# Stick-breaking attention: the mask's products ahead of the scores', and one product for two sums

## The chip, the cores and the metric

One core of a Trainium2 chip runs the whole program. The metric is device time in microseconds (us) of one execution, the median of several runs; lower is better. TensorE (PE in the profile) does matrix products, VectorE (DVE) and ScalarE (ACT) work on elements, GpSimd (POOL) does some element work and issues some transfers, SyncE (SP) issues the others. PSUM is the memory that TensorE writes its sums to, in banks of 512 fp32 columns.

## The reference

Two layers of a transformer-like trunk over 512 frames and 16 meta tokens of width 1024: half a SwiGLU, then a mixer (stick-breaking attention with 8 heads of 64 beside a convolution branch), then half a SwiGLU. The change touches the attention alone:

```python
def stick_breaking_attention(q, k, v):
    """A[t,s] = sigmoid(z_ts) * prod_{s<j<t} (1 - sigmoid(z_tj)), s < t."""
    ...
    def block(args):
        qb, start = args
        z = jnp.einsum('bhqd,bhkd->bhqk', qb, kh) * scale
        qpos = start + jnp.arange(Q_BLOCK, dtype=jnp.int32)[:, None]
        valid = key_pos < qpos
        log_keep = jnp.where(valid, jax.nn.log_sigmoid(-z), 0.0)
        after = lax.cumsum(log_keep, axis=3, reverse=True) - log_keep
        attn = jnp.where(valid, jnp.exp(jax.nn.log_sigmoid(z) + after), 0.0)
        return jnp.einsum('bhqk,bhkd->bhqd', attn, vh)
```

## The kernel before, in words

Activations lie with channels on the 128 partitions and the 528 tokens along the columns. Large fp32 products are made of three products of parts: a number is split into a rounded part and a rest (`qh`, `ql`), and high by high, high by rest and rest by high are summed in PSUM.

The mixer of a layer takes the heads in four pairs, `attend(i, ...)`. While a pair is worked on, TensorE's gaps are filled with the projections that come next: `attend` is a generator, and at each of its `yield`s the loop around it puts half of a projection (24 products of `by_halves`, line 700) into TensorE's stream. That engine's order is fixed by the order of the calls (`tc.manual_schedule`). The other engines' instructions are ordered by the framework, by priority.

The 528 keys are the 512 of four blocks of 128 (t = 3, 2, 1, 0) and the last 16, which are handled apart, as a corner. For one pair `attend` does, in TensorE's order:

- the corner: scores of the 16 last keys with the 16 last queries (and of the first 16 keys with the first 16 queries, in the layer that keeps the meta tokens) in the tile `zs` of 64 used rows: rows 0 to 15 for the pair's first head, rows 32 to 47 for its second; their softplus is `e4` (64x32);
- at line 895 a product of `e4` with the first 128 columns of the constant `l4` adds the sums over later keys to `zs`, and puts the first head's total over the 16 keys into row 127 (column 127 of `l4` is -1 for that head); at line 896 a second product, with the other 128 columns of `l4`, puts the second head's total into row 127 of columns 32 to 47 and nothing else; a copy on DVE (line 900) takes rows 96 to 127 of both to the tile `corner`;
- `scores(t, ...)` four times, for pieces 3, 2, 1 and 0 of the keys, with 256, 272, 400 and 512 queries: the three products of parts for each of the two heads (line 852), and then for each head the mask's product (line 855), identity by a bf16 mask of 240, 128, 128 and 112 columns. The softplus follows on ACT and DVE, and for t = 3 `corner` is subtracted (line 862). In the text these are the first, second, third and fourth piece;
- between them other products: line 907 (`vb` by `a4`, after the first piece, only where the meta tokens are kept), line 919 (the same two operands' corner values, right ahead of the third piece), the sums over later blocks (lines 874 to 877) and the values (line 892).

A head is 64 channels, so the score products contract over 64 rows: the first head of the pair lies on partitions 0 to 63, the second on 64 to 127. The trace writes such a product as 64*128 (64 rows by 128 columns of the array) and one that uses all rows as 128*128. The products of lines 895, 896, 907 and 919 are plain fp32, contract over partitions 0 to 63, and show as two passes each. The mask's product is 128*128, as are the projections.

All constants come in one tile `cc`; `l4` is a view of it in the kernel before (line 297). `constants()` copies others of them to tiles of their own, at a late priority. A PSUM accumulation starts with the product that has `start=True`; the later ones of the same bank add to what has been written since, and overwrite elsewhere.

Of the kernel before, what the change touches and what calls it, by code (L numbers as in the profile page):

```python
# [7 lines left out]
F32 = mybir.dt.float32  # L8
# [5 lines left out]
P = 128  # L14
# [40 lines left out]
C_L4 = 496  # L55
# [5 lines left out]
def kernel(ctx, tc, hT, par, const, wg1, wu1, wd1, win, wao, wco, wout, wg2, wu2, wd2, out):  # L61
    nc = tc.nc
    act, dve, pool, pe = nc.scalar, nc.vector, nc.gpsimd, nc.tensor

    cst = ctx.enter_context(tc.tile_pool(name="cst", bufs=1))
# [11 lines left out]
    def split(x, hi, lo):  # L77

        act.copy(hi, x)  # L79
        dve.tensor_tensor(out=lo, in0=x, in1=f(hi), op=ALU.subtract)  # L80

    @contextmanager
    def priority(offset):

        old = tc.cur_priority
        tc.cur_priority = max(0, old + offset)
        yield
        tc.cur_priority = old
# [7 lines left out]
    def fn(out, in_, func, **kw):  # L96
        need = SETS[func]
        if table["set"] != need:
            load = act.preload_act_table_set(need)
            for p in table["acts"]:  # L100
                tc.add_manual_dep(load.ins, p.ins.name, NOSYNC, reason="table order")
            table.update(set=need, load=load, acts=[])
        i = act.activation(out, in_, func, **kw)
        tc.add_manual_dep(i.ins, table["load"].ins.name, NOSYNC, reason="table order")
        table["acts"].append(i)
# [137 lines left out]
    def unit(*key):  # L243
        while state["prep"] < min(len(units), state["use"] + 1 + LOOK):
            if units[state["prep"]][2] in QUAD and quads["pool"] is None:
                break
            prep_unit()
        assert units[state["use"]][0] == key, (units[state["use"]][0], key)
        state["use"] += 1
        return ready.pop(key)  # L250
# [25 lines left out]
    cc = cst.tile([P, N_CONST], F32, name="cc")  # L276
# [6 lines left out]
    identb = cst.tile([P, P], BF16, name="identb")  # L283
    maskb = cst.tile([P, 240], BF16, name="maskb")
    masksb = cst.tile([64, 32], BF16, name="masksb")

    def constants():

        nc.sync.dma_start(prm[:, N_NORM:], par[:, N_NORM:])
        nc.sync.dma_start(cc, const)  # L290
        with priority(LATE):
            dve.tensor_copy(trir, cc[:, C_TRI:C_TRI + P])
            dve.tensor_copy(identb, ident)
            dve.tensor_copy(maskb, cc[:, C_MASK:C_MASK + 240])
            dve.tensor_copy(masksb, cc[:64, C_MS:C_MS + 32])

    l4 = cc[:64, C_L4:C_L4 + 2 * P]
    bias = cst.tile([P, 4], F32, name="bias")
    pool.memset(bias[:, 0:1], 1e-6)
    pool.memset(bias[:, 1:2], 1e-5)  # L300
# [153 lines left out]
    def ffn(l, fi, st, mode, after):  # L454
# [3 lines left out]
        with tc.tile_pool(name=f"ffn{l}{fi}", bufs=1, reuse_waits="tile") as fp, \  # L458
# [53 lines left out]
            def first_head():  # L512
# [5 lines left out]
                for a, b in BEGIN:  # L518
                    for k in range(a, b):
                        prepare(fp, k, 0, st, alloc="later")  # L520
                    for raw, (hi, lo) in zip(begin, ws):
                        split(raw[:, a:b], hi[:, a:b], lo[:, a:b])
                    for k in range(a, b):
                        squares(fp, k, st, mode)
                    if b == KD:
                        fetch()
                        fetch_sums()
                        constants()
                        norm["r"] = rms_rstd(fp, st, ptile("pe"), mode)
                    for k in range(a, b):  # L530
                        xh, xl = st["u"][k]
                        for ps, (hi, lo) in zip(pss, ws):
                            for pi, (wt, xt) in enumerate(((hi, xh), (hi, xl), (lo, xh))):
                                for e, s in enumerate(toks):
                                    pe.matmul(ps[:, e, :TH], wt[:, k, :], xt[:, s], start=(k == 0 and pi == 0),
                                              stop=(k == KD - 1 and pi == 2))
# [121 lines left out]
    def mixer(l, st, omode, after):  # L658
        last = omode == XO
        with ExitStack() as es:  # L660
# [8 lines left out]
            def hold(k, width, name):  # L669
                return hpool.tile([P, width], F32R, tag=f"h{k}", bufs=1, name=name)  # L670
# [62 lines left out]
            with tc.tile_pool(name=f"psm{l}", bufs=2, space=bass.MemoryType.PSUM, reuse_waits="tile") as psp, \  # L733
                    tc.tile_pool(name=f"psz{l}", bufs=2, space=bass.MemoryType.PSUM, reuse_waits="tile") as psz:

                def ztile():
                    return psz.tile([P, 2, 512], F32, tag="z", name="z")
# [28 lines left out]
                with tc.tile_pool(name=f"att{l}", bufs=1, reuse_waits="tile") as ap_:  # L766
# [26 lines left out]
                    def softplus(dst, z, np_):  # L793
                        act.activation(dst, z, AF.Abs)
                        fn(dst, dst, AF.Exp, bias=bias[:np_, 3:4], scale=-1.0)
                        fn(dst, dst, AF.Ln, bias=bias[:np_, 2:3], scale=1.0)
                        dve.scalar_tensor_tensor(out=dst, in0=z, scalar=0.0, in1=dst, op0=ALU.max, op1=ALU.add)

                    def attend(i, step, qf, kf, vf):
                        qc = META if last else 0  # L800
                        qh, ql, kh, kl = (hold(n, T, nm) for n, nm in enumerate(("qh", "ql", "kh", "kl")))
# [5 lines left out]
                        w = ncor * 16  # L807
                        zt = ztile()
                        zs, pt = zt[:, 0, :], zt[:, 1, :]
# [7 lines left out]
                        for c, t0 in ((0, SEQ), (1, 0))[:ncor]:  # L817
                            for hh in range(2):
                                r = slice(64 * hh, 64 * hh + 64)
                                pe.matmul(zs[32 * hh:32 * hh + 16, c * 16:c * 16 + 16], kf[r, t0:t0 + 16],  # L820
                                          qf[r, t0:t0 + 16], start=False, stop=False, skip_group_check=True)
                        e4 = ap_.tile([64, 32], F32, tag="e4", bufs=2, name="e4")
# [22 lines left out]
                        def scores(t, q0, n, m0):  # L845
                            z = ztile()
                            ks = slice(t * P, (t + 1) * P)

                            for pi, (kk, qq) in enumerate(((kh, qh), (kh, ql), (kl, qh))):
                                for hh in range(2):  # L850
                                    r = slice(64 * hh, 64 * hh + 64)
                                    pe.matmul(z[:, hh, :n], kk[r, ks], qq[r, q0:q0 + n], start=(pi == 0), stop=False,  # L852
                                              skip_group_check=True)
                            for hh in range(2):
                                pe.matmul(z[:, hh, :240 - m0], identb, maskb[:, m0:], start=False, stop=False,
                                          skip_group_check=True)
                            sp = ap_.tile([P, 2, 512], F32, tag="big", bufs=BIG, name="sp")[:, :, :n]
                            sh, sl = (ap_.tile([P, 2, n], F32R, tag=f"s{x}{t}" if t else "big", bufs=1 if t else BIG,
                                               name=f"s{x}") for x in "hl")
                            softplus(sp, z[:, :, :n], P)  # L860
                            if t == 3:
                                dve.tensor_tensor(out=sp[96:128, :, n - 16:], in0=sp[96:128, :, n - 16:],
                                                  in1=corner[96:128], op=ALU.subtract)
                            split(sp, sh, sl)
                            later[t] = (z, sh, sl, q0, n)
# [26 lines left out]
                                    pe.matmul(po[:, hh, q0 - META:q0 - META + n], v[:, t, hh * P:hh * P + P], p[:, hh, :],  # L892
                                              start=False, stop=(t == 0 and p is al), skip_group_check=True)

                        pe.matmul(zs[:, :w], l4[:, 0:P], e4[:, :w], start=False, stop=True, skip_group_check=True)
                        pe.matmul(zs[:, 32:48], l4[:, P:2 * P], e4[:, :16], start=True, stop=True, skip_group_check=True)
                        fn(a4[:, :w], zs[:64, :w], AF.Exp, bias=bias[:64, 3:4])
                        corner = ap_.tile([P, 2, 16], F32, tag="corner", bufs=2, name="corner")
                        zc = zs[96:128, 0:64].rearrange("p (a b) -> p a b", a=2)[:, :, :16]
                        dve.tensor_copy(corner[96:128], zc)  # L900
                        scores(*PIECES[0])
                        yield
                        step(2)
                        oh = bp.tile([P, T], F32R, tag=f"oh{i}", bufs=1, name="oh")
                        ol = bp.tile([P, T], F32R, tag=f"ol{i}", bufs=1, name="ol")
                        if not last:
                            pe.matmul(zs[:, 64:80], vb[:, 2, :], a4[:, 16:32], start=True, stop=True, skip_group_check=True)
                            with priority(-EARLY):
                                act.copy(oh[:, :META], zs[:, 64:80])
                                dve.tensor_tensor(out=ol[:, :META], in0=zs[:, 64:80], in1=f(oh[:, :META]),  # L910
                                                  op=ALU.subtract)
                        yield
                        scores(*PIECES[1])
                        yield
                        sums_and_weights(3)
                        yield
                        po = psz.tile([P, 2, 512], F32, tag="o", bufs=1, name="po")
                        for hh in range(2):
                            pe.matmul(po[:, hh, 496:512], vb[:, hh, :], a4[:, :16], start=True, stop=False,
                                      skip_group_check=True)  # L920
# [38 lines left out]
                    with tc.manual_schedule(engines={mybir.EngineType.PE}):  # L959
                        for i in range(4):  # L960
                            for _ in attend(i, step, *parts(i)):
                                next(beside, None)
                        for n, fill in enumerate(FILL_END):
                            for _ in range(fill):
                                next(beside, None)
                            step(n)
                        for _ in beside:
                            pass

            with tc.tile_pool(name=f"post{l}", bufs=1, reuse_waits="tile") as pp, \  # L970
# [64 lines left out]
                for jj in range(4):  # L1035
                    w = unit("co", l, jj)
# [85 lines left out]
```

## Time and profile before

| | |
|---|---|
| median of three runs | 2159.0 us (2158.93 to 2159.9) |
| the profiled execution | 2159.58 us |
| its span in the trace | 2157.8 us |
| granted TensorE clock, mean | 0.999 |
| PE busy | 2141.5 us, 99% |
| PEld (weight loads) busy | 2055.4 us, 95% |
| DVE busy | 1521.7 us, 71% |
| ACT busy | 1151.1 us, 53% |
| POOL busy | 485.1 us, 22% |

A record of a product is longer than the distance to the next one, since products overlap in the array; what a product costs in a stream is the distance between starts.

### The profile page before, as it was taken

To read this page: it belongs to the slowest core of one execution; us is meant where nothing else is said; L and a number is where in the kernel's file an instruction comes from. 1 tells how busy PE (TensorE), PEld (TensorE's weight loads), DVE (VectorE), ACT (ScalarE), POOL (GpSimd) and SP (SyncE) were. 2 spreads that over 40 slices of the span, in tenths; PEclk is the share of its full clock that TensorE was granted. 3 is DMA by queue.
4 is the path that set the end of the run, shared out by engine and by line. 5 is a ranking of instruction groups with operands and counts; after the bars stand their busy time and mean duration, and the time that the engine had idled before them with its cause. 6 is when DMAs were issued, how large, how long until landed. Compare 5 with 4: busy or idle time off the path is not lost. (4 is left out here: it accounts for less than half of the span.)

```text
span 2157.8 us, 39881 instructions
## 1 busy us (share of the span) xinstructions
PE 2141.5 (99%) x16242; PEld 2055.4 (95%) x16242; DVE 1521.7 (71%) x2076; ACT 1151.1 (53%) x1590; POOL 485.1 (22%) x429
## 2 busy tenths in 40 slices
PE   9999999999999999999999999999999999999998
PEld 8999999999999999999999999999888879999897
DVE  7867685677766767677877676856677767767685
ACT  6434355477767535343554343554778685444354
POOL 1322321211111131323113223212112111322320
PEclk9999999999999999999999999999999999999999
DMA  8465547865677647464365655368655876665532
GB/s 237 136 166 140 137 107 201 178 133 120 134 171 180 172 129 188 128 164 118 96 171 144 166 143 141 103 197 181 144 123 135 184 184 166 159 177 144 141 111 76
DMA packets 140168, 324.90 MB, mean 151 GB/s; under 512 B 15568, under 2 KB 19664, under 8 KB 139984
## 3 DMA queue, kind: packets, MB, share of 16 engines
q1 hardware_dynamic: 101856, 226.36, 32.9%
q0 software_dynamic: 37440, 95.44, 26.1%
q8 instruction: 127, 2.08, 0.4%
q10 hardware_dynamic: 688, 0.55, 0.1%
q14 instruction: 57, 0.47, 0.1%
HBM read 315.86 MB, written 6.42 MB: 149 GB/s over the span
## 5 line engine op out<-in xcount | busy, mean ns | idle before, releaser
L79 ACT CAST wh<-wr 128x1024 fp32r<-128x1024 f32 (+4 forms) x275 | 243.5, 888 | 377.6 <-PE ps L259 93.5
L80 DVE TENSOR_TENSOR wl<-wr,wh 128x1024 fp32r<-128x1024 f32 (+4 forms) x275 | 300.1, 1094 | 59.0 <-ACT wh L79 55.3
L79 ACT CAST wh<-s 128x1024 fp32r<-128x1024 f32 x158 | 165.8, 1049 | 275.1 <-DVE s L236 91.2
L80 DVE TENSOR_TENSOR wl<-s,wh 128x1024 fp32r<-128x1024 f32 x158 | 214.9, 1360 | 59.5 <-ACT wh L79 58.8
L700 PE MATMUL ps<-uh,wh 128*128 128x264 f32 (+1 forms) x792 | 244.2, 308 | 0.0
L700 PE MATMUL ps<-uh,wl 128*128 128x264 f32 (+1 forms) x792 | 240.0, 303 | 0.0
L700 PE MATMUL ps<-ul,wh 128*128 128x264 f32 (+1 forms) x792 | 239.9, 303 | 0.0
L621 POOL TENSOR_TENSOR h<-h,dt 128x528 f32<-128x528 f32 (+1 forms) x96 | 181.0, 1891 | 256.0 <-DVE dt L619 253.3
L210 POOL DMA_DIRECT2D s<-wg x78 | 74.7, 970 | 592.4 <-DMA s<-wg 202.1
L728 DVE SCALAR_TENSOR_TENSOR y<-uc,prm,y 128x528 f32<-128x528 f32 (+1 forms) x240 | 197.6, 823 | 4.1
L224 ACT CAST wh<-wr 128x1024 fp32r<-128x1024 f32 x104 | 109.1, 1049 | 140.4 <-issue 47.1
L561 PE MATMUL ps<-ul,wh 128*128 128x264 f32 (+1 forms) x624 | 177.4, 284 | 0.0
L561 PE MATMUL pb<-sl,wh 128*128 128x264 f32 (+1 forms) x624 | 176.9, 283 | 0.0
L561 PE MATMUL ps<-uh,wl 128*128 128x264 f32 (+1 forms) x624 | 176.8, 283 | 0.0
L561 PE MATMUL pb<-sh,wl 128*128 128x264 f32 (+1 forms) x624 | 176.8, 283 | 0.0
L561 PE MATMUL pb<-sh,wh 128*128 128x264 f32 (+1 forms) x624 | 176.5, 283 | 0.0
L561 PE MATMUL ps<-uh,wh 128*128 128x264 f32 (+1 forms) x624 | 176.2, 282 | 0.0
L700 PEld LDWEIGHTS ps<-uh,wl 128*128 128x128 f32 x792 | 149.1, 188 | 5.9
L700 PEld LDWEIGHTS ps<-uh,wh 128*128 128x128 f32 x792 | 148.9, 188 | 5.5
L700 PEld LDWEIGHTS ps<-ul,wh 128*128 128x128 f32 x792 | 149.0, 188 | 5.2
L259 PE MATMUL ps<-al,wh 128*128 128x264 f32 (+1 forms) x616 | 142.3, 301 | 0.5 <-DVE al L80 0.2
L259 PE MATMUL ps<-ah,wh 128*128 128x264 f32 (+1 forms) x616 | 141.8, 300 | 0.0
(312 smaller groups left out, 6472.5 us busy)
## 6 DMA issues: line engine op xcount, KB each, us to landing
wr<-wd SPq DMA_DIRECT2D x96, 384.0 KB, 3.4
wr<-win SPq DMA_DIRECT2D x72, 512.0 KB, 4.1
wl<-win POOLq DMA_DIRECT2D x72, 512.0 KB, 7.8
wr<-wg SPq DMA_DIRECT2D x117, 256.0 KB, 3.0
wr<-wu SPq DMA_DIRECT2D x117, 256.0 KB, 3.4
s<-wg SPq DMA_DIRECT2D x78, 256.0 KB, 5.0
s<-wu SPq DMA_DIRECT2D x78, 256.0 KB, 5.6
s<-wg POOLq DMA_DIRECT2D x78, 256.0 KB, 5.4
```

Source lines behind the costliest of these rows:

```text
L79: act.copy(hi, x)
L80: dve.tensor_tensor(out=lo, in0=x, in1=f(hi), op=ALU.subtract)
L210: pool.dma_start(t[:, a:b], src, accum_op=ALU.add)
L224: act.copy(hi[:, :nk], raw[:, :nk])
L259: pe.matmul(ps[:, c, :n], wt[:, k0 + k, :], xt[:, s:s + n], start=(k == 0 and pi == 0), stop=(k == nk - 1 and pi == 2))
L561: pe.matmul(ps[:, e, :TH], wt[:, 4 * e + kk, :], xt, start=start and kk == 0 and pi == 0, stop=kk == 3 and pi == 2, skip_group_check=True)
L621: pool.tensor_tensor(out=tri(h[j], mode), in0=tri(h[j], mode), in1=tri(t, mode), op=ALU.add)
L700: pe.matmul(ps, wt[:, k, :], xt[:, s], start=(n == 0 and pi == 0), stop=(n == KD - 1 and pi == 2))
L728: t = dve.scalar_tensor_tensor(out=y, in0=uc[i][:, c0 + k:k + T], scalar=col(w0 + k), in1=y, op0=ALU.mult, op1=ALU.add)
```

## The change

In `scores` the two mask products now come first and start the accumulation (`start=True`), and the six products of parts add to it. The second product with `l4` is gone: `l4` becomes a tile of 64x128 of its own, a copy of the first 128 columns with column 95 replaced by the second head's column of -1, so that one product leaves the first head's total in row 127 and the second head's in row 95, both in columns 0 to 15. `corner` is then filled by two copies of 32x16, from rows 96 to 127 and from rows 64 to 95. Two copies that build `l4` join `constants()`.

```diff
         with priority(LATE):
             dve.tensor_copy(trir, cc[:, C_TRI:C_TRI + P])
+            dve.tensor_copy(l4, cc[:64, C_L4:C_L4 + P])
+            dve.tensor_copy(l4[:, 95:96], cc[:64, C_L4 + 2 * P - 1:C_L4 + 2 * P])
             dve.tensor_copy(identb, ident)
...
-    l4 = cc[:64, C_L4:C_L4 + 2 * P]
+
+    l4 = cst.tile([64, P], F32, name="l4")
...
-
-                            for pi, (kk, qq) in enumerate(((kh, qh), (kh, ql), (kl, qh))):
+                            for hh in range(2):
+                                pe.matmul(z[:, hh, :240 - m0], identb, maskb[:, m0:], start=True, stop=False,
+                                          skip_group_check=True)
+
+                            for kk, qq in ((kh, qh), (kh, ql), (kl, qh)):
                                 for hh in range(2):
                                     r = slice(64 * hh, 64 * hh + 64)
-                                    pe.matmul(z[:, hh, :n], kk[r, ks], qq[r, q0:q0 + n], start=(pi == 0), stop=False,
+                                    pe.matmul(z[:, hh, :n], kk[r, ks], qq[r, q0:q0 + n], start=False, stop=False,
                                               skip_group_check=True)
-                            for hh in range(2):
-                                pe.matmul(z[:, hh, :240 - m0], identb, maskb[:, m0:], start=False, stop=False,
-                                          skip_group_check=True)
...
-                        pe.matmul(zs[:, :w], l4[:, 0:P], e4[:, :w], start=False, stop=True, skip_group_check=True)
-                        pe.matmul(zs[:, 32:48], l4[:, P:2 * P], e4[:, :16], start=True, stop=True, skip_group_check=True)
+                        pe.matmul(zs[:, :w], l4, e4[:, :w], start=False, stop=True, skip_group_check=True)
                         fn(a4[:, :w], zs[:64, :w], AF.Exp, bias=bias[:64, 3:4])
                         corner = ap_.tile([P, 2, 16], F32, tag="corner", bufs=2, name="corner")
-                        zc = zs[96:128, 0:64].rearrange("p (a b) -> p a b", a=2)[:, :, :16]
-                        dve.tensor_copy(corner[96:128], zc)
+                        for hh in range(2):
+                            dve.tensor_copy(corner[96:128, hh], zs[96 - 32 * hh:128 - 32 * hh, :16])
```

The order on TensorE, in the first layer's second pair. At the first piece, before (`po` is the values' sum of the pair ahead, `z<-e,cc` are the two products with `l4`, x2 is one row for the two heads; the row pair of the mask comes a second time in place of the dots):

```order
L892 MATMUL po<-al,v 128x400
L895 MATMUL z<-e_5746,cc 128x32
L896 MATMUL z<-e_5746,cc 128x16
L852 MATMUL z<-qh,kh 128x256 x2
L852 MATMUL z<-ql,kh 128x256 x2
L852 MATMUL z<-qh,kl 128x256 x2
L855 LDWEIGHTS identb
L855 MATMUL z<-maskb,identb 128x240
...
L700 MATMUL ps<-uh_4162,wh 128x264
```

The same place in the changed kernel (its line 898 is 895 of before, 852 the masks, 858 the products of parts, 895 the values, 703 the projections):

```order
L895 MATMUL po<-al,v 128x400
L898 MATMUL z<-e_5749,l_122 128x32
L852 LDWEIGHTS identb
L852 MATMUL z<-maskb,identb 128x240
...
L858 MATMUL z<-qh,kh 128x256 x2
L858 MATMUL z<-ql,kh 128x256 x2
L858 MATMUL z<-qh,kl 128x256 x2
L703 MATMUL ps<-uh_4165,wh 128x264
```

The second product with `l4` is gone, and the masks stand between the first one and the products of parts.

At the third piece, before, with the corner's values (line 919) ahead of it:

```order
L919 MATMUL po<-a_5747,vb 128x16 x2
L852 MATMUL z<-qh,kh 128x400 x2
L852 MATMUL z<-ql,kh 128x400 x2
L852 MATMUL z<-qh,kl 128x400 x2
L855 LDWEIGHTS identb
L855 MATMUL z<-maskb,identb 128x128
...
L700 MATMUL ps<-uh_4162,wh 128x264
```

The same place now:

```order
L921 MATMUL po<-a_5750,vb 128x16 x2
L852 LDWEIGHTS identb
L852 MATMUL z<-maskb,identb 128x128
...
L858 MATMUL z<-qh,kh 128x400 x2
L858 MATMUL z<-ql,kh 128x400 x2
L858 MATMUL z<-qh,kl 128x400 x2
L703 MATMUL ps<-uh_4165,wh 128x264
```

Here too the masks part two runs of 64*128 products that stood next to each other. At the second and the fourth piece, 128*128 products stand on both sides before and after; there the masks only change sides. The same holds in all four pairs of both layers. On DVE one copy to `corner` has become two in each pair, and two copies join the constants'; the order of ACT, POOL and SP is as before.

## Rows read from the trace of the kernel before

**Rows 1.** The page's part 1: busy time, share of the span, instructions.

```profile
PE 2141.5 (99%) x16242; PEld 2055.4 (95%) x16242; DVE 1521.7 (71%) x2076; ACT 1151.1 (53%) x1590; POOL 485.1 (22%) x429
```

**Rows 2.** Busy us of the engines from 430 to 600 us, and PE's waits there.

```profile
430.00:600.00 170.00, 169.84 (x1368) 159.39 (x1367) 133.32 (x204) 130.12 (x192) 31.34 (x31) 1.00 0.59 130
PE z L895 <- ACT vb L837: 0.2, 1, 0.2
```

**Rows 3.** PE in order of time, second piece, first pair: start us, us, operation.

```profile
447.80 0.28 PE L700 MATMUL ps<-ul,wh 128*128 128x264 f32 x1
447.92 0.28 PE L700 MATMUL ps<-uh,wl 128*128 128x264 f32 x1
448.13 0.40 PE L852 MATMUL z<-qh,kh 64*128 64x272 f32 x2
448.36 0.29 PE L852 MATMUL z<-ql,kh 64*128 64x272 f32 x2
448.49 0.28 PE L852 MATMUL z<-qh,kl 64*128 64x272 f32 x2
448.71 0.29 PE L855 MATMUL z<-maskb,identb 128*128 128x128 bf16 x2
...
449.01 0.29 PE L700 MATMUL ps<-ul,wh 128*128 128x264 f32 x1
```

**Rows 4.** PE in order of time around line 907 of the first pair.

```profile
444.68 0.39 PE L907 MATMUL z<-a,vb 64*128 64x16 f32 x2
445.00 0.39 PE L700 MATMUL ps<-uh,wh 128*128 128x264 f32 x1
445.23 0.28 PE L700 MATMUL ps<-ul,wh 128*128 128x264 f32 x1
```

**Rows 5.** PE in order of time, first piece of the second pair.

```profile
482.86 0.40 PE L895 MATMUL z<-e,cc 64*128 64x32 f32 x2
483.00 0.38 PE L852 MATMUL z<-qh,kh 64*128 64x256 f32 x1
483.10 0.37 PE L896 MATMUL z<-e,cc 64*128 64x16 f32 x2
...
483.53 0.27 PE L852 MATMUL z<-ql,kh 64*128 64x256 f32 x1
483.64 0.28 PE L852 MATMUL z<-qh,kl 64*128 64x256 f32 x1
483.85 0.38 PE L855 MATMUL z<-maskb,identb 128*128 128x240 bf16 x2
...
484.20 0.28 PE L700 MATMUL ps<-ul,wh 128*128 128x264 f32 x1
```

**Rows 6.** PE in order of time, third piece of the first pair.

```profile
455.30 0.39 PE L919 MATMUL po<-a,vb 64*128 64x16 f32 x2
...
455.54 0.37 PE L919 MATMUL po<-a,vb 64*128 64x16 f32 x2
...
456.04 0.33 PE L852 MATMUL z<-ql,kh 64*128 64x400 f32 x1
456.21 0.34 PE L852 MATMUL z<-qh,kl 64*128 64x400 f32 x1
456.49 0.29 PE L855 MATMUL z<-maskb,identb 128*128 128x128 bf16 x2
...
456.79 0.28 PE L700 MATMUL ps<-ul,wh 128*128 128x264 f32 x1
```

**Rows 7.** Groups of PE by shape, 430 to 600 us: busy us, mean ns of one.

```profile
L855 PE MATMUL z<-maskb,identb 128*128 128x128 bf16 x16 | 2.3, 224 | 0.0
L855 PE MATMUL z<-maskb,identb 128*128 128x240 bf16 x8 | 1.5, 272 | 0.0
```

**Rows 8.** DVE in order of time: the constants' end, and `corner` in the first pair.

```profile
37.79 0.71 DVE L497 TENSOR_TENSOR g<-ps,rstd 128x528 f32<-128x528 f32 x1 [0.95 <-PE ps L487]
442.27 0.20 DVE L900 COPY corner<-z 32x32 f32<-32x32 f32 x1
444.62 0.69 DVE L797 SCALAR_TENSOR_TENSOR sp<-z,sp 128x512 f32<-128x512 f32 x1 [2.16 <-ACT sp L103]
```

## The prediction, made before the changed kernel ran

> **What bounds the kernel now.** I read the busy shares first: PE is busy 99% of the span and its weight loads 95%, while DVE, ACT and POOL have room [rows 1]. An average could hide a stage that waits, so the attention of the first layer comes next. From 430 to 600 us PE is busy 169.84 of 170.00 us, and the only wait listed for it there is 0.2 us in all [rows 2]. So what counts in that stretch is how densely TensorE's products follow each other, and the busy figure cannot tell that, since a record of 0.28 us stands for a product that is followed by the next one after 0.12 us. I therefore read distances between starts in order of time.
>
> Four prices come out of that, of which the third is the one that matters. I call a product that the trace writes as 128*128 full and one written as 64*128 half.
>
> - In a stream of full projections the starts lie 447.92 - 447.80 = 0.12 us apart, and a half pair (two heads side by side) follows a half pair after 448.49 - 448.36 = 0.13 us [rows 3].
> - From a full product to the first half pair it is 448.13 - 447.92 = 0.21 us, and from there to the next pair 448.36 - 448.13 = 0.23 us instead of 0.13. Entering the half form thus costs 0.09 + 0.10 = 0.19 us beyond the products themselves [rows 3].
> - From half to full: the masks start 448.71 - 448.49 = 0.22 us after the last half pair [rows 3]; behind the two passes of line 907 the first projection starts 445.00 - 444.68 = 0.32 us after the first pass, and the second projection 0.23 us after that instead of 0.12 [rows 4]. Leaving costs about as much as entering.
> - In each of these a product of the other form starts 0.06 to 0.08 us before the end of the last record of the old form: 447.92 + 0.28 - 448.13 = 0.07, 448.49 + 0.28 - 448.71 = 0.06 [rows 3], 444.68 + 0.39 - 445.00 = 0.07 [rows 4]. So the array is let run nearly empty at each change of form, whatever the length of the product. I use 0.07.
>
> There is also something that half products get for free. In the first piece a product of parts (483.00) starts between the plain fp32 products of lines 895 (482.86) and 896 (483.10): the second head's parts, on the other 64 rows, run beside the first head's rows [rows 5].
>
> **The change part by part.** I count per piece from one fixed start to the second projection behind the piece, once as the rows have it and once put together from the prices.
>
> Where the masks go, I need their cost inside a full stream, which no row shows: before, they always stand right behind a change of form. Bounds: the two short masks (128 columns) start 0.29 - 0.224 = 0.07 us apart, and the long ones (240 columns) 0.38 - 0.272 = 0.11 us [rows 3, 5, 7]; from above, a projection's 0.12 us. I take 0.07 and 0.11, as they are rows of the same instruction, and keep 0.12 for the range. After the masks the half form starts 0.224 - 0.07 = 0.15 us behind the second short one, or 0.272 - 0.07 = 0.20 us behind the long one [rows 7].
>
> *Second and fourth piece.* Before, from the last projection to the second one behind: 449.01 - 447.92 = 1.09 us [rows 3]. Now: projection to mask 0.12, mask to mask 0.07, mask to parts 0.15, parts 0.23 and 0.13, parts to projection 0.22, and 0.23 to the second [rows 3, 4]: 1.15 us. That is +0.06 us, because before the masks' short records hid in the filling of the array. The fourth piece has the same pattern with more columns. 16 pieces (two in each of four pairs of two layers): **+1.0 us**.
>
> *First piece.* Before, from line 895: 484.20 - 482.86 = 1.34 us [rows 5]. Gone: the two passes of line 896, 483.10 - 482.86 = 0.24 us if read from the two passes ahead of them. New: the masks need all rows, so the parts of the second head can no longer run beside the fp32 passes, and there is a change to full and one back. Put together: two passes to mask 0.32 [rows 4], mask to mask 0.11, mask to parts 0.20, parts 0.23 [rows 3] and 483.64 - 483.53 = 0.11, parts to projection 483.85 - 483.64 = 0.21 [rows 5], 0.23 to the second [rows 4]: 1.41 us. So the product that is saved is paid back: +0.07 us, 8 pieces: **+0.6 us**.
>
> *Third piece.* Here nothing is saved. Before, from line 919: 456.79 - 455.30 = 1.49 us [rows 6]. Now: four passes to mask 0.32 + 0.24 (the second two as 455.54 - 455.30), 0.07, 0.15, parts 0.27 (0.17 for 400 columns, from 456.21 - 456.04, and 0.10 for entering) and 0.17, parts to projection 456.49 - 456.21 = 0.28, and 0.23 [rows 3, 4, 6, 7]: 1.73 us. +0.24 us, 8 pieces: **+1.9 us**.
>
> *DVE.* One 32x32 copy of 0.20 us becomes two of 32x16: at most 0.20 us more for each of 8 pairs, 1.6 us if it had no cover. Its cover is DVE's idle time of 2.16 us behind that copy, in which it waits for ACT [rows 8]; what reads `corner` comes after that. The two copies that build `l4` stand among the constants' copies, with 0.95 us of waiting for PE close behind them [rows 8]; without that cover at most 0.4 us, once (two such copies at 0.20). Both at nothing.
>
> *The path.* PE has no waits to give back in the stretch, so its time goes to the end. Moving the masks first brings no earlier start either, since PE does not wait at the pieces. Sum: 1.0 + 0.6 + 1.9 = **+3.5 us**, 0.16%. The profiled execution is 2159.58 us with a span of 2157.8 us; against it the sum gives 2163.1 and 2161.3 us. The median of the runs is 0.6 us lower, so the forecast is 2159.0 + 3.5 = **2162.5 us**. About 0.2%, or 4.3 us, is what a measurement of this kernel can tell from no change, so this lies just inside it. Its own range, with 0.1 us of reading error in each of 32 pieces partly cancelling, is 2161 to 2164 us.
>
> **A rule weighed.** At 447.92 to 448.13 us the half form's weights are not in the array when the projection has streamed [rows 3]. The Trainium skill, "TensorE: Matmul & The Clock Gate", section "Step-by-step: what each phase is for", says that weight loads are pulled ahead of products in flight where the row groups don't conflict or the background buffer takes them. By that, entering the half form behind a mask would cost nothing and the sum would be -2.6 us (first rival); by the rows, which show the cost at every entry, it is +3.5 us. The same page, "Back-to-back issue gap", gives about 81 ns for a product of 128 columns in a stream; with that in place of 0.07 us the 48 shorter masks would add 0.5 us to the sum. No row here shows a short product in such a stream.
>
> **The rivals.**
> 1. *The half form's weights load beneath the masks.* The masks are short and bf16, and if their own load frees the path early, the 0.19 us for entering go in all 32 pieces: -6.1 us, 3.5 - 6.1 = -2.6, 2156.4 us. For it: parts do overlap with other rows' passes [rows 5]. Against it: behind full products the entry shows it each time. Chance 0.07.
> 2. *Changes of form are priced alike wherever they stand, and the masks only change sides.* Then only line 896's passes count: 8 x -0.24 = -1.9, 2157.1 us. This is also the case that the reordering does nothing. Against it: the first and the third piece get two more changes each, and rows 3 and 4 show a price for every one. Chance 0.12.
> 3. *Slower: a mask in a full stream costs a projection's slot.* Its place is the step from the projection's fp32 weights to the bf16 weights of the mask: if that load, not the 128 columns, sets the distance, 48 short masks cost 0.12 instead of 0.07 us and 16 long ones 0.12 instead of 0.11: 2.4 + 0.2 us more, +6.1 in all, 2165.1 us. It decides from about 0.09 us for a short mask, where the sum passes 4.3 us. For it: a projection of 264 columns takes no more than 0.12 us, so loads cannot be far from setting the pace, with weight loads busy 95% [rows 1, 3]. Against it: the two masks behind the change of form start 0.07 us apart [rows 7]. Chance 0.17.
>
> **How the numbers follow.** The forecast has 0.59, the rivals 0.07, 0.12 and 0.17, and 0.05 stay for a wait that nothing here shows. The first two rivals lie within 0.2% as well. A quarter of the forecast's own chance lies above 2163.3 us. Slower by over 0.2%: 0.15 + 0.17, less a little for a light third rival: 0.31. Faster by over 0.2%: 0.03, only from a still better first rival or the unknown. Within: 0.66. The range takes in the forecast, the second and the third rival: 2157.0 to 2165.5 us.
>
> **What would show it.** Right: the mask's rows 0.2 us or more behind the passes of lines 898 and 921, no product of parts beside those passes, and a third piece some 0.2 us longer from line 921 to the second projection. PE still without waits, and its count of products 16 lower. Third rival: masks 0.12 us behind each other. First rival: parts that follow the mask after 0.07 to 0.1 us and each other after 0.13. Wrong altogether: a new wait of PE at the masks, or DVE late with `corner`.

## The result and the profile after

| | before | after |
|---|---|---|
| median | 2159.0 us (2158.24 to 2159.9, 21 runs) | 2162.49 us (2161.79 to 2163.3, 21 runs) |
| ratio, 95% interval | | 1.0016 (1.0011 to 1.0022) |
| span of the profiled execution | 2157.8 us | 2160.9 us |

The change costs 3.5 us, 0.16%: slower, clear of zero by its interval, and just inside the 0.2% that were called no change beforehand.

The busy line of the changed kernel's page, the counterpart of [rows 1]: 16 fewer PE records (8 products of two passes), 3.5 us more of PE, and the other engines within 1 us.

```profile
PE 2145.0 (99%) x16226; PEld 2056.4 (95%) x16226; DVE 1521.9 (70%) x2086; ACT 1151.7 (53%) x1590; POOL 484.5 (22%) x429
```

PE's waits over the whole span in the changed kernel (engine, line, who was waited for, us in total, times, longest). There is none at the masks (line 852 now); the one of line 898 is that of [rows 2].

```profile
PE ps L538 <- ACT wh L79: 4.8, 1, 4.8
PE ps L689 <- ACT yh L79: 0.8, 2, 0.7
PE ps L259 <- DVE al L80: 0.2, 1, 0.2
PE z L898 <- ACT vb L840: 0.2, 1, 0.2
```

PE in order of time in the changed kernel (start us, us, operation): the second piece of the first pair, the counterpart of [rows 3].

```profile
448.09 0.28 PE L703 MATMUL ps<-uh,wl 128*128 128x264 f32 x1
448.21 0.29 PE L852 MATMUL z<-maskb,identb 128*128 128x128 bf16 x2
448.43 0.40 PE L858 MATMUL z<-qh,kh 64*128 64x272 f32 x2
448.66 0.28 PE L858 MATMUL z<-ql,kh 64*128 64x272 f32 x2
448.79 0.28 PE L858 MATMUL z<-qh,kl 64*128 64x272 f32 x2
449.00 0.39 PE L703 MATMUL ps<-uh,wh 128*128 128x264 f32 x1
449.23 0.28 PE L703 MATMUL ps<-ul,wh 128*128 128x264 f32 x1
```

From the last projection to the second behind: 1.14 us, against 1.09 before. The masks follow the projection after 0.12 us like any product of the stream, so a change of number type alone (the masks are bf16) has no price of this kind. The price of a change of form stands on either side of the parts: ahead of them it is 0.22 us from the first mask to the first parts (0.15 from the second mask, which starts 0.29 - 0.224 = 0.07 us behind the first), and then 0.23 to the next parts; behind them it is 0.21 and 0.23.

PEld (weight loads) in order of time at the same place:

```profile
448.21 0.12 PEld L852 LDWEIGHTS <-identb 128*128 128x128 bf16 x2
448.43 0.19 PEld L858 LDWEIGHTS z<-qh,kh 64*128 64x128 f32 x2
```

The load for the first parts starts only with its own product (448.43): it is not pulled ahead of the masks. That alone proves little, since the masks' load starts with its product too (448.21), at no extra cost; e6 below has the cleaner pair.

The same view at the first piece of the second pair, the counterpart of [rows 5]:

```profile
483.38 0.41 PE L898 MATMUL z<-e,l 64*128 64x32 f32 x2
483.72 0.38 PE L852 MATMUL z<-maskb,identb 128*128 128x240 bf16 x2
...
484.57 0.39 PE L703 MATMUL ps<-uh,wh 128*128 128x264 f32 x1
484.80 0.29 PE L703 MATMUL ps<-ul,wh 128*128 128x264 f32 x1
```

No product of parts starts among the fp32 passes any more, and the masks come 0.34 us after the first pass. 1.42 us from line 898 to the second projection, with two passes; before it was 1.34 with four.

And at the third piece of the first pair, the counterpart of [rows 6]:

```profile
455.53 0.61 PE L921 MATMUL po<-a,vb 64*128 64x16 f32 x4
456.07 0.28 PE L852 MATMUL z<-maskb,identb 128*128 128x128 bf16 x2
456.29 0.45 PE L858 MATMUL z<-qh,kh 64*128 64x400 f32 x2
456.58 0.34 PE L858 MATMUL z<-ql,kh 64*128 64x400 f32 x2
...
457.03 0.39 PE L703 MATMUL ps<-uh,wh 128*128 128x264 f32 x1
457.25 0.28 PE L703 MATMUL ps<-ul,wh 128*128 128x264 f32 x1
```

1.72 us against 1.49, with the same products.

DVE in order of time in the changed kernel, the counterpart of [rows 8]: the two copies take 0.37 us together, out of the same gap.

```profile
37.84 0.71 DVE L500 TENSOR_TENSOR g<-ps,rstd 128x528 f32<-128x528 f32 x1 [0.94 <-PE ps L490]
442.34 0.37 DVE L902 COPY corner<-z 32x16 f32<-32x16 f32 x2
444.71 0.69 DVE L800 SCALAR_TENSOR_TENSOR sp<-z,sp 128x512 f32<-128x512 f32 x1 [2.01 <-ACT sp L103]
```

### The profile page after: what moved, and what is told of

Its sections match the earlier page's. It is cut to its first block, busy times and chain, and to the rows that moved or that the text cites. A ratio compares the mean times of both kernels' runs of the same rounds, so it can differ in the third digit from the quotient of the medians.

```text
span 2160.9 us, 39849 instructions
## 1 busy us (share of the span) xinstructions
PE 2145.0 (99%) x16226; PEld 2056.4 (95%) x16226; DVE 1521.9 (70%) x2086; ACT 1151.7 (53%) x1590; POOL 484.5 (22%) x429
```

## The experiments

Each kernel was timed beside the kernel before on the same chip; differences are against those runs, whose median was 2159.39 us for the first four and 2159.06 us for the last two.

**e1, one product only.** From the changed kernel, with `scores` as before:

```diff
-                            for hh in range(2):
-                                pe.matmul(z[:, hh, :240 - m0], identb, maskb[:, m0:], start=True, stop=False,
-                                          skip_group_check=True)
...
+                            for hh in range(2):
+                                pe.matmul(z[:, hh, :240 - m0], identb, maskb[:, m0:], start=False, stop=False,
+                                          skip_group_check=True)
```

> The one product with l4 and the two copies to corner, as in the change; the mask's products stay behind the products of parts, as before. Theory (each change between 64-row and 128-row products costs about 0.2 us of TensorE's time beyond the products): nothing is parted, so the saved product of two passes counts in full, 0.22 to 0.24 us in each of 8 pairs: -1.8 us, 2157.2 us against 2159.0. Rival (the one product, its own l4 tile or the two copies cost the time, by a wait on VectorE): the same as the change or more, 2159 to 2162.5 us.

Measured: 2157.56 us, -1.8 us, ratio 0.9991 (0.9982 to 1.0). The interval just reaches 1, so the time alone does not settle it; PE's rows at the first piece of the second pair do:

```profile
482.97 0.29 PE L898 MATMUL z<-e,l 64*128 64x32 f32 x1
482.98 0.38 PE L855 MATMUL z<-qh,kh 64*128 64x256 f32 x1
...
483.74 0.38 PE L858 MATMUL z<-maskb,identb 128*128 128x240 bf16 x2
```

0.77 us from line 898 to the masks, against 0.99 before [rows 5]: the saved product counts in full, and the second head's first part (482.98) starts beside the first pass. The new tile and the second copy cost nothing that can be seen.

**e2, masks first only.** From the kernel before:

```diff
+                            for hh in range(2):
+                                pe.matmul(z[:, hh, :240 - m0], identb, maskb[:, m0:], start=True, stop=False,
+                                          skip_group_check=True)
...
-                            for hh in range(2):
-                                pe.matmul(z[:, hh, :240 - m0], identb, maskb[:, m0:], start=False, stop=False,
-                                          skip_group_check=True)
```

> The masks ahead of the parts, but both products with l4 as before. Theory: second and fourth pieces +0.05 us each (16 of them), third pieces +0.23 us, first pieces, now with four fp32 passes that run alone ahead of the masks, +0.31 us: 0.8 + 1.8 + 2.5 = +5.1 us, 2164.1 us. Rival (the order of products costs nothing, only their number counts): 2159.0 us.

Measured: 2164.61 us, +5.2 us, ratio 1.0024 (1.0015 to 1.0033). The order alone costs more than the whole change, with exactly the products of before. PE at the first piece of the second pair:

```profile
483.62 0.41 PE L895 MATMUL z<-e,cc 64*128 64x32 f32 x2
483.87 0.37 PE L896 MATMUL z<-e,cc 64*128 64x16 f32 x2
484.17 0.38 PE L849 MATMUL z<-maskb,identb 128*128 128x240 bf16 x2
484.48 0.39 PE L855 MATMUL z<-qh,kh 64*128 64x256 f32 x2
```

Line 896 is paid in full here: it is 0.55 us from line 895 to the masks, against 0.34 from line 898 to them in the changed kernel, 0.21 us for its two passes. e1 and e2 add up to the change: -1.8 + 5.2 = +3.4 us.

**e3, masks ahead of the passes too.** From the changed kernel: the two mask products become a function `masks`, which the first and the third piece call ahead of the fp32 products.

```diff
+                        z0 = masks(PIECES[0][3])
                         pe.matmul(zs[:, :w], l4, e4[:, :w], start=False, stop=True, skip_group_check=True)
...
-                        scores(*PIECES[0])
+                        scores(*PIECES[0], z0)
...
                         po = psz.tile([P, 2, 512], F32, tag="o", bufs=1, name="po")
+                        z2 = masks(PIECES[2][3])
...
-                        scores(*PIECES[2])
+                        scores(*PIECES[2], z2)
```

> As the changed kernel, but in the first and the third piece the two mask products also stand ahead of the fp32 passes with l4 and of the corner's values, so that those passes and the parts stand next to each other again. Theory: the two extra changes of form of these pieces go; what is left is 0.05 us in 24 pieces for masks that lead, and in the first pieces the saved product, -0.23 + 0.07 us: 1.2 - 1.3 = about 0, 2159.0 us (3.4 below the change). Rival (a mask that leads a piece costs by itself, 5.3 us over 32 pieces or 0.17 us each, wherever the passes stand): as the changed kernel, 2162.5 us.

Measured: 2159.26 us, -0.1 us, ratio 1.0 (0.9991 to 1.0009). The masks still lead every piece, and the changed kernel's loss of 3.5 us is gone. PE at the third piece of the first pair:

```profile
454.07 0.29 PE L851 MATMUL z<-maskb,identb 128*128 128x128 bf16 x2
454.28 0.39 PE L926 MATMUL po<-a,vb 64*128 64x16 f32 x2
454.42 0.44 PE L861 MATMUL z<-qh,kh 64*128 64x400 f32 x1
454.53 0.37 PE L926 MATMUL po<-a,vb 64*128 64x16 f32 x2
...
455.47 0.39 PE L703 MATMUL ps<-uh,wh 128*128 128x264 f32 x1
```

The parts stand among the passes again (454.42). So what costs most is not that the masks lead, but that they part two runs of the same form. A mask that leads still costs 0.05 us a piece (the table below), 1.6 us over 32 pieces, about what the saved product gives.

**e4, masks between the parts.** From the kernel before:

```diff
                             for pi, (kk, qq) in enumerate(((kh, qh), (kh, ql), (kl, qh))):
+                                for hh in range(2 if pi == 2 else 0):
+                                    pe.matmul(z[:, hh, :240 - m0], identb, maskb[:, m0:], start=False, stop=False,
+                                              skip_group_check=True)
...
-                            for hh in range(2):
-                                pe.matmul(z[:, hh, :240 - m0], identb, maskb[:, m0:], start=False, stop=False,
-                                          skip_group_check=True)
```

> The kernel before with the masks between the second and the third product of parts: two more changes of form in each of the 32 pieces, nothing else. Theory: the second piece put together from the rows takes 0.21 + 0.23 + 0.22 + 0.07 + 0.15 + 0.33 + 0.23 = 1.44 us against 1.09, +0.35 us in each of 32 pieces: +11.2 us, 2170.2 us. Rival (only the number of products counts): 2159.0 us. Second rival (only the overlap of fp32 passes with parts matters, not the changes themselves): at most the first and third pieces grow, by under 4 us.

Measured: 2170.4 us, +11.0 us, ratio 1.005 (1.0037 to 1.0062). PE at the second piece of the first pair, where no fp32 pass is near:

```profile
447.97 0.28 PE L700 MATMUL ps<-uh,wl 128*128 128x264 f32 x1
448.19 0.40 PE L855 MATMUL z<-qh,kh 64*128 64x272 f32 x2
448.42 0.29 PE L855 MATMUL z<-ql,kh 64*128 64x272 f32 x2
448.64 0.29 PE L851 MATMUL z<-maskb,identb 128*128 128x128 bf16 x2
448.85 0.39 PE L855 MATMUL z<-qh,kl 64*128 64x272 f32 x2
...
449.40 0.28 PE L700 MATMUL ps<-ul,wh 128*128 128x264 f32 x1
```

1.43 us against 1.09: two more changes of form cost 0.34 us though nothing here has lost an overlap. The second rival of this run falls with it.

To see where the time lies in all of these, I took for every piece of all eight pairs the distance from the last product ahead of it to the second one behind, less that of the kernel before (mean us per piece; the sum is over 32 pieces):

| kernel | first | second | third | fourth | sum | measured |
|---|---|---|---|---|---|---|
| the change | +0.07 | +0.05 | +0.24 | +0.05 | +3.3 | +3.5 |
| e1 | -0.22 | 0.00 | 0.00 | 0.00 | -1.7 | -1.8 |
| e2 | +0.29 | +0.05 | +0.25 | +0.05 | +5.1 | +5.2 |
| e3 | -0.17 | +0.05 | +0.05 | +0.05 | -0.1 | -0.1 |
| e4 | +0.38 | +0.34 | +0.34 | +0.33 | +11.1 | +11.0 |

The distances in TensorE's stream account for each measured difference to 0.2 us. The intervals of the times are wider than that, 1 to 3 us on either side, so this shows that nothing else is needed, and not that nothing else moved.

**e5, the corner's mask over 128 rows.** This and the next run go after changes of form that the kernel before has too. From e1:

```diff
-    masksb = cst.tile([64, 32], BF16, name="masksb")
+    masksb = cst.tile([P, 32], BF16, name="masksb")
...
-            dve.tensor_copy(masksb, cc[:64, C_MS:C_MS + 32])
+            dve.tensor_copy(masksb, cc[:, C_MS:C_MS + 32])
...
-                        pe.matmul(zs[:, :w], identb[:64, :], masksb[:, :w], start=True, stop=False, skip_group_check=True)
+                        pe.matmul(zs[:, :w], identb, masksb[:, :w], start=True, stop=False, skip_group_check=True)
```

> e1 (one product with l4, masks behind the parts) with one change of form taken away in each pair: the corner's mask product, 64 rows in all kernels so far, stands between transposes of 128 rows and the corner's scores; its bf16 mask gets 128 rows (the added ones are zero), so that it follows the transposes without a change. Theory: 0.20 us from transpose to mask becomes about 0.11, 8 pairs: -0.7 us against e1, so 2.5 us below the kernel before, 2156.5 us if that is at 2159.0. Rival (a change costs only where score products of two heads overlap with something): as e1, 1.8 below the kernel before.

Measured: 2156.62 us, -2.4 us, ratio 0.9988 (0.9979 to 0.9997); 0.6 us below e1 by the two differences, where 0.7 were forecast, though a step of that size between two such intervals is not shown by the times alone. The rows show it. PE in the first pair, first of the kernel before, then of e5:

```profile
436.24 0.60 PE L815 MATMUL z<-cc,v 128*128 128x128 f32 x4
436.77 0.19 PE L816 MATMUL z<-masksb,identb 64*128 64x32 bf16 x1
436.89 0.27 PE L820 MATMUL z<-q,k 64*16 64x16 f32 x8
437.09 0.39 PE L700 MATMUL ps<-uh,wh 128*128 128x264 f32 x1
```

```profile
436.18 0.60 PE L818 MATMUL z<-cc,v 128*128 128x128 f32 x4
436.61 0.18 PE L819 MATMUL z<-masksb,identb 128*128 128x32 bf16 x1
436.72 0.27 PE L823 MATMUL z<-q,k 64*16 64x16 f32 x8
436.92 0.39 PE L703 MATMUL ps<-uh,wh 128*128 128x264 f32 x1
```

From the first transpose to the mask it is 0.43 us in place of 0.53, and the gain is kept up to the projection behind: 0.74 in place of 0.85. Eight pairs at 0.10 us make 0.8 us; the first pair's wait for ACT at line 898 takes 0.1 of it back (0.3 us, 0.2 in [rows 2]).

The reason expected is shown only in part. By rows no change is gone: it has moved from ahead of the mask to behind it, where the corner's scores follow with 64 rows. There it adds nothing: the scores start 0.11 to 0.12 us behind the mask in both kernels, in both 0.07 us before the end of its record, which is short (0.18 us, a transpose's 0.27). Whether the step from mask to scores (64*128 to 64*16) was a change already, or the change is cheaper behind a shorter product, no run separates.

**e6, the lone passes over 128 rows.** From e5:

```diff
-                        a4 = ap_.tile([64, 32], F32, tag="a4", bufs=2, name="a4")
+                        a4 = ap_.tile([P, 32], F32, tag="a4", bufs=2, name="a4")
...
-                        vb = ap_.tile([64, 3, P], F32, tag="vb", bufs=2, name="vb")
+                        vb = ap_.tile([P, 3, P], F32, tag="vb", bufs=2, name="vb")
...
-                        fn(a4[:, :w], zs[:64, :w], AF.Exp, bias=bias[:64, 3:4])
+                        fn(a4[:, :w], zs[:, :w], AF.Exp, bias=bias[:, 3:4])
...
-                            pe.matmul(po[:, hh, 496:512], vb[:, hh, :], a4[:, :16], start=True, stop=False,
+                            pe.matmul(po[:, hh, 496:512], vb[:64, hh, :], a4[:64, :16], start=True, stop=False,
```

> e5, and also the lone product of the meta tokens' values (line 907 of the kernel before, 64 rows, projections on both sides) made 128 rows: a4 is computed for all 128 rows of its source (finite numbers in the added rows) and vb holds zeros there. Two changes of form go in each of the 4 pairs of the first layer, and the number of products is the same. Theory: from the last projection to the second behind 444.46 to 445.23, 0.77 us, becomes four slots of 0.12, 0.48 us: -0.29 us in 4 pairs, -1.2 us against e5, so 3.7 us below the kernel before, 2155.3 us if that is at 2159.0. Rival (the 0.22 us behind the passes is the latency of fp32 passes, not the change of form): no gain against e5.

Measured: 2155.59 us, -3.5 us, ratio 0.9984 (0.9976 to 0.9993), the fastest of all; 1.0 us below e5 where 1.2 were expected, again a step that the times alone do not show. PE in the first pair, in e6:

```profile
443.66 0.29 PE L703 MATMUL ps<-uh,wl 128*128 128x264 f32 x1
443.79 0.29 PE L909 MATMUL z<-a,vb 128*128 128x16 f32 x2
443.93 0.37 PE L703 MATMUL ps<-uh,wh 128*128 128x264 f32 x1
444.13 0.29 PE L703 MATMUL ps<-ul,wh 128*128 128x264 f32 x1
```

The same two fp32 passes of 16 columns, with twice the rows, half of them zero: 0.47 us from the last projection to the second behind, where it was 0.77 in the kernel before (the expectation has its rows). The rival, latency of the fp32 passes, falls: they follow 0.13 us behind the projection, and the next projection starts 0.14 us after the first of them, against 0.32 in [rows 4].

The loads of the same product, first in the kernel before, then in e6:

```profile
444.67 0.29 PEld L907 LDWEIGHTS z<-a,vb 64*128 64x128 f32 x2
```

```profile
443.67 0.31 PEld L909 LDWEIGHTS z<-a,vb 128*128 128x128 f32 x2
```

With 64 rows behind a projection the load starts 0.01 us ahead of its product (444.68 in [rows 4]); with 128 rows it starts 0.12 us ahead (443.79), beside the projection.

## Why the prediction was right

The forecast was 2162.5 us and 2162.49 us were measured; that it fits to the hundredth is luck, since its own range was 2161 to 2164 us. The terms are the better test:

- *Second and fourth piece*, forecast +1.0 us in 16 pieces at 0.06: measured 0.05, 0.8 us. The masks inside the stream cost what was taken, 0.07 us apart (0.29 - 0.224; a mask's record is again 0.224 us in the mean), and 0.12 behind the projection; the dearer figure for a short product that the prediction weighed is not what two masks in a row show.
- *First piece*, forecast +0.6 us: measured +0.07 each, 0.6 us. e1 and e2 show the two halves that the sum netted out: -0.22 for the product saved, +0.29 for the order.
- *Third piece*, forecast +1.9 us: measured +0.24 each, 1.9 us. e3 takes it down to +0.05.
- *DVE and the path*, forecast at nothing: the gap behind the copies is 2.01 us instead of 2.16, no wait was added, and e1 has all of DVE's part of the change without a loss.
- *The rule weighed.* In the changed kernel the parts follow the first mask after 0.22 us (448.21 to 448.43), the second after 0.15, and each other after 0.23. The pull-ahead of weight loads that the Trainium skill states ("TensorE: Matmul & The Clock Gate", "Step-by-step: what each phase is for") is there in e6, where the lone product's load starts 0.12 us ahead of it, and does not reach across the change of form: with 64 rows the same load starts with its product. What holds is the sentence of another page of the Trainium skill, "TensorEngine Tiling (Array Packing)", section "Key Properties": a change of tiling mode drains the engine. e4 and e6 agree with it and give it a price that the page doesn't have, 0.34 us (e4) and 0.77 - 0.47 = 0.30 us (e6) for two changes.

The first rival wanted the parts 0.07 to 0.1 us behind the masks; they start 0.14 to 0.15 us behind the second of the short ones in all 24 pieces that have them. The second, that only the number of products counts, holds for e1 and fails in e2 by 5 us. The third, a mask at a projection's slot, is refuted by the 0.07 us above. The range of 2157.0 to 2165.5 us was wide beside what the rows allowed; the second rival had no row behind it.

One point stays half open: a change costs 0.17 us in e4 and 0.15 in e6, but in the third piece two more of them cost 0.24 - 0.05 = 0.19 us, 0.10 each. Most of the gap can be read in the kernel before, from the parts that start behind line 919's passes:

```profile
455.77 0.43 PE L852 MATMUL z<-qh,kh 64*128 64x400 f32 x1
```

The next parts of that head follow after 0.27 us (456.04) and the last after 0.17 [rows 6]. So the longer first step, 0.10 us of the price of entering, was paid there already, without a change of form, and the changed kernel pays it once too (456.29 to 456.58, 0.29 us). Why it is paid behind those passes, no run shows.

## What to carry to other kernels

Where the matrix engine is busy 99% and waits for nothing, read distances between starts, not busy time, and look for the places where products over 64 rows and over 128 rows meet: here such a meeting costs 0.1 to 0.2 us, as much as one or two products, and least behind a short product (e5). So group the products by form before taking any away, and give a lone small product the form of its neighbours by padding its rows with zeros, which cost no time here (e6); a product that is saved by splitting such a group is paid back at once.

## What the runs showed of the hardware that I had not expected

- In e3 the first pair's first piece fell by more than the others', from 1.79 to 1.43 us in the distance of the table, where the other pairs of that layer fell from 1.61 to 1.48: the masks ahead of line 902 cover its wait for ACT, which is the 0.2 us of [rows 2].
- The two row halves start side by side in e1: the second head's first part starts 0.01 us after the first fp32 pass (482.97 and 482.98), while before it started 0.14 us after it [rows 5]. There it even starts (483.00) ahead of line 896's passes (483.10), which come before it in TensorE's order; so it does in all 8 pairs.
